# A state-space layer on one core: where the diagonal term, the zero fills and four norm vectors are loaded and issued, and the order of the stage's operations

## The chip, the cores and the metric

The kernel runs on one core of a Trainium2 chip. The metric is device time in microseconds (us) of one execution. A core has five engines that run side by side and wait for each other only through semaphores: TensorE (PE), VectorE (DVE), ScalarE (ACT), GpSimd (POOL) and SyncE (SP). Each works off its own queue in order. In this kernel SP issues nearly all loads; POOL issues the transfers that add to their destination.

## The reference

The model is one S5 state-space layer with a GLU and an MLP, then a shared key and value projection, one forgetting-attention layer with its MLP, and a final norm, on 512 tokens of 1024 channels in float32. The change lies in the first of these:

```python
def s5_mixer(u, log_dt, a_re, a_im, b_re, b_im, c_re, c_im, d_skip, w_glu):
    uf = u.reshape(bsz, length, N_GROUPS, SSM_GROUP)          # 64 groups of 16 channels
    lam_bar = jnp.exp(lam * dt)                                # 64 complex states in a group
    b_bar = ((lam_bar - 1.0) / lam)[..., None] * b
    bu = jnp.einsum('blgc,gpc->blgp', uf, b_bar)
    _, states = lax.associative_scan(_ssm_binop, (a_elems, bu), axis=1)
    y = jnp.real(jnp.einsum('blgp,gcp->blgc', states, c))
    y = y + d_skip.reshape(N_GROUPS, SSM_GROUP) * uf           # the diagonal term
    z = jax.nn.gelu(y.reshape(bsz, length, D_MODEL))
    zw = z @ w_glu
    return zw[..., :D_MODEL] * jax.nn.sigmoid(zw[..., D_MODEL:])
```

The input u of this function is the normalised x: x times its inverse root mean square times the vector mix_norm[0].

## The kernel before, in words

The sequence is cut into 64 chunks of 8 tokens (T = 8). Inside a chunk the layer is a small Toeplitz matrix over 8 tokens and 16 channels; between chunks a scan carries the state. The 64 groups are worked in 8 blocks (b = 0 to 7) of 8 groups.

A part in front of the blocks, in the order of the code, loads the parameters, builds the powers of lam_bar (LL, ML) and the transposed B and C (XY, four planes). Planes 1 and 3 of XY are planes 0 and 2 with the upper and lower 64 partitions exchanged; SP does that with two DMAs each (lines 344 and 345, `swap`), for groups 0 to 15 (`sw_0_0`, `sw_2_0`) and for the rest (`sw_0_1`, `sw_2_1`). VectorE multiplies plane 0 by the norm vector first (line 470, `gain`).

Then come the blocks' operations. Their order is written out by hand in the string ORDER, one name per operation with its block; each engine takes its own share of that list in order, so the list is the order of every queue. The names that matter here:

- LR, mR, gR, tk, rxv: VectorE's last preparations (powers, their products with the coefficients, the gain for groups 16 to 63, the angles' tables, the inverse root mean square rxy). xs: ScalarE scales x by rxy into xs.
- gn: TensorE transposes the tile gl (four norm vectors of later layers), ScalarE copies it to gains.
- win1, win2, wina and wo1, wo2, woa: for a block the matrices Win and Wout, two products on VectorE each and an addition by a DMA that POOL issues (line 348).
- u, us: transposes of xs on TensorE and their copies. pw, wt: transposes of Win and copies to WinT. pd: the chunks' inputs to the state. tab0, tab3, tabn: tables of cosines and sines (CS).
- pt, ks, kd, kw, tr: the block's Toeplitz matrix. pt multiplies on TensorE, ks copies it to ks, kd adds the diagonal term dgb (line 614, VectorE), kw writes it to a DRAM buffer (line 617), tr reads it back as a Toeplitz matrix with a shifting access pattern (line 625). The DRAM buffer has seven blocks of zeros in front, which kzero writes once (line 262).
- cd, da, scan, pp, padd: the scan between chunks. cd rotates into cc (one buffer); da exchanges halves, for blocks 0 to 3 with two matmuls, for blocks 4 to 7 with a pair of POOL's adding DMAs; scan is one VectorE instruction; pp rotates back; padd is a pair of adding DMAs.
- py1, py2: TensorE applies the Toeplitz matrix and Wout. gelu, zt, zh, lo: the activation, its transposes and the split into two float32r parts.
- gl_n, gs, gv, gp: three of the GLU's weight chunks are loaded, split and multiplied inside this stage.

ks needs pt, and kd needs dgb. dgb holds d_skip times mix_norm[0] on the diagonal places of a block: two sets of four small loads by SP (line 253, tiles dgb and dgg) and, as operation dg of the list, two VectorE multiplies.

The buffers for Wout come from two pairs A and B; the string WQ says which pair each takes. After the stage the rest of the GLU (line 834), the MLPs and the attention follow; their order is made by a planner that fills gaps of the list with matmuls that are ready.

Of the kernel before, what the change touches and what calls it, by code (L numbers as in the profile page):

```python
# [1592 lines left out]
```

## Time and profile before

| what | us |
|---|---|
| median of 3 runs | 1198.26 |
| lowest, highest | 1196.67, 1198.49 |
| the profiled execution's own time | 1196.73 |
| its span, from the first to the last instruction | 1195.0 |
| TensorE busy in the span | 1113.5 |
| VectorE busy | 908.3 |
| ScalarE busy | 588.5 |
| GpSimd busy | 291.4 |

The span is what the trace shows; the time of an execution holds 1.73 us more. A busy time counts an engine's instructions, not its waits. The state-space stage is the first eighth of the span: the last block's py2 starts at 148.63 us.

### The profile page before, as it was taken

The page shows a single profiled execution, that of the slowest core. Times are in us where ns is not written, and L with a number is a line of the kernel's source. Part 1 is how long each engine was busy: PE and PEld are TensorE (multiplying, and loading weights), DVE is VectorE, ACT ScalarE, POOL GpSimd, SP SyncE. Part 2 cuts the span into 40 slices and gives each one's busy share as a digit, 9 for nine tenths or more (in the row PEclk, how much of TensorE's full clock was granted, in tenths as well). Part 3 has the DMA queues.
Part 4 walks back from the last instruction along what each step waited for, and adds up shares of the span by engine and source line. Part 5 has one row for each costly group of instructions (what it writes and reads, how often), then busy time and mean ns, then how long its engine had stood idle before and what let it go on. Part 6 is the DMA issues. An engine that isn't in the chain of part 4 may idle for free.

```text
span 1195.0 us, 19068 instructions
## 1 busy us (share of the span) xinstructions
PE 1113.5 (93%) x7205; PEld 985.7 (82%) x7205; DVE 908.3 (76%) x1640; ACT 588.5 (49%) x1072; POOL 291.4 (24%) x290
## 2 busy tenths in 40 slices
PE   1687899999999999999999999888899999999997
PEld 1566778899899898998888999767889898999986
DVE  7988438899877777768566778885979877778754
ACT  4656355455434444436345666554755444443433
POOL 3134214422121212203002222314442312213101
PEclk9989999999999999999999999998999999999999
DMA  7889743142323323234145444311143323232222
GB/s 157 181 176 207 188 144 106 53 141 90 123 89 102 111 75 120 88 103 128 55 132 134 107 107 137 94 54 53 36 126 104 112 83 124 89 119 93 89 88 71
DMA packets 118140, 131.19 MB, mean 110 GB/s; under 512 B 15200, under 2 KB 98432, under 8 KB 118048
## 3 DMA queue, kind: packets, MB, share of 16 engines
q1 hardware_dynamic: 113824, 118.44, 33.6%
q0 software_dynamic: 4224, 11.54, 5.5%
q8 instruction: 57, 0.93, 0.3%
q14 instruction: 35, 0.29, 0.1%
HBM read 103.21 MB, written 3.60 MB: 89 GB/s over the span
## 4 chain that ended last, share of the span: by engine, by line
PE 75%; DVE 11%; DMA 5%; ACT 3%; SPq 3%; issue 2%; POOL 1%; DVEq 0%; ACTq 0%; POOLq 0%
PE pu L943 23%; PE po L834 16%; PE pvs L1508 14%; PE pk L834 6%; PE pv L834 6%; PE pvs L1154 2%; PE po L1292 2%; DMA PP<-PP 1%; DMA cc<-cc 1%; DMA st<-in_mlp_w_dram 1%; PE ptp L1258 1%; PE pf L1142 1%; DVE prob L1253 1%; DMA TW<-kd 1%; PE pw L834 1%
## 5 line engine op out<-in xcount | busy, mean ns | idle before, releaser
L943 PE MATMUL pu<-hm,ar 128*128 128x256 f32 x1536 | 229.0, 284 | 5.1 <-ACT hm L887 2.2
L943 PEld LDWEIGHTS pu<-hm,ar 128*128 128x128 f32 x1536 | 204.1, 193 | 6.7 <-ACT hm L887 2.6
L922 POOL TENSOR_TENSOR ar<-ar,st 128x256 f32<-128x256 f32 x62 | 81.8, 1320 | 414.2 <-DVE ar L918 373.1
L124 ACT ACTIVATE wt<-st 128x1024 fp32r<-128x1024 f32 x110 | 116.3, 1057 | 124.6 <-PE pu L943 27.2
L834 PE MATMUL po<-at,wt 128*128 128x512 f32 x768 | 176.9, 389 | 0.0
L1508 PE MATMUL pvs<-wt,at 128*128 128x512 f32 (+1 forms) x768 | 175.5, 388 | 0.0
L834 PEld LDWEIGHTS po<-at,wt 128*128 128x128 f32 x768 | 143.2, 188 | 29.1
L1508 PEld LDWEIGHTS pvs<-wt,at 128*128 128x128 f32 x768 | 142.6, 188 | 28.8
L128 DVE TENSOR_TENSOR wt<-st,wt 128x1024 fp32r<-128x1024 f32 x90 | 116.9, 1298 | 36.9 <-ACT wt L124 36.8
L943 PE MATMUL pu<-hd,x 128*128 128x256 f32 x768 | 136.0, 284 | 0.0
L911 ACT ACTIVATE ar<-ar 128x512 fp32r<-128x512 f32 x128 | 77.0, 627 | 91.6 <-PE pu L943 78.5
L943 PEld LDWEIGHTS pu<-hd,x 128*128 128x128 f32 x768 | 113.2, 192 | 2.9 <-issue 0.5
L912 DVE TENSOR_TENSOR ar<-ar 128x512 fp32r<-128x512 f32 x128 | 87.9, 692 | 31.4 <-ACT ar L911 31.3
L128 POOL TENSOR_TENSOR wt<-st,wt 128x1024 fp32r<-128x1024 f32 x20 | 48.2, 2410 | 143.7 <-ACT wt L124 133.9
L911 ACT ACTIVATE x<-st 128x512 fp32r<-128x512 f32 x62 | 36.4, 625 | 94.8 <-PE pvs L1508 45.0
L918 DVE TENSOR_TENSOR ar<-st 128x512 f32<-128x512 f32 x62 | 49.8, 806 | 39.3 <-DMA st<-in_mlp_w_dram 38.8
L834 PE MATMUL pv<-zt,wt 128*128 128x512 f32 x312 | 74.3, 397 | 0.4 <-ACT hT L1016 0.4
L834 PEld LDWEIGHTS pv<-zt,wt 128*128 128x128 f32 x312 | 59.2, 192 | 12.9 <-ACT hT L1016 0.6
L1244 ACT ACTIVATE prob<-psx,mx 128x128 f32<-128x128 f32 (+1 forms) x64 | 33.8, 529 | 60.5 <-DVE mx L1242 60.5
L1063 ACT ACTIVATE at<-c 128x512 fp32r<-128x512 f32 x64 | 39.8, 630 | 42.9 <-DVE c L1061 42.9
L923 POOL TENSOR_TENSOR ar<-ar,st 128x256 f32<-128x256 f32 x62 | 58.7, 950 | 4.2
L1049 DVE TENSOR_TENSOR hT<-hT,po 128x512 f32<-128x512 f32 x64 | 43.4, 679 | 16.1 <-PE po L834 16.1
(338 smaller groups left out, 1997.6 us busy)
## 6 DMA issues: line engine op xcount, KB each, us to landing
st<-in_mlp_w_dram SPq DMA_DIRECT2D x126, 512.0 KB
st<-in_ssm_w_glu_dram SPq DMA_DIRECT2D x16, 512.0 KB
st<-in_w_kvf_dram SPq DMA_DIRECT2D x14, 512.0 KB
hx<-kt SPq DMA_DIRECT2D x48, 128.0 KB
Win<-tB POOLq DMA_DIRECT2D x8, 512.0 KB, 5.5
TW<-tB POOLq DMA_DIRECT2D x8, 512.0 KB, 6.4
TW<-kd SPq DMA_DIRECT2D x32, 128.0 KB
st<-in_attn_wq_dram SPq DMA_DIRECT2D x8, 512.0 KB
```

The source lines that it names most:

```text
L124: S.activation(wt[:, 0], st, AF.Copy)
L128: (G if slot[1] == "A" and CFG["x"][7 + lows[0] % 3] == "G" else V).tensor_tensor(wt[:, 1], st, wt[:, 0].bitcast(F32), op=ALU.subtract)
L834: TE.matmul(pts[m], wt[:, a, k, m * P:(m + 1) * P], acts[k0 + k][:, b], start=(first and k0 == parts[0][0] and k == 0 and n == 0), stop=(k ...
L911: S.activation(X[0], src, AF.Copy)
L912: V.tensor_tensor(X[1], src, X[0].bitcast(F32), op=ALU.subtract)
L918: V.tensor_tensor(Ta[:, :, js].rearrange("p w j n -> p j w n"), f[:, :, 1:3], f[:, :, 0:1].broadcast_to([P, 2, 2, P]), op=ALU.add)
L922: e.tensor_tensor(Tb[:, 0, js], Ta[:, 0, js], v[:, :, 1, 0], op=ALU.add)
L923: e.tensor_tensor(Tb[:, 1, js], Tb[:, 0, js], v[:, :, 1, 1], op=ALU.add)
L943: TE.matmul(self.acc[p], self.W[p][:, a, j], self.H.moving(p, j, b), start=(p == g[0] and j == 0 and n == 0), stop=(p == g[-1] and j == 3 ...
L1049: V.tensor_tensor(hT[:, m, :], hT[:, m, :], po[j], op=ALU.add)
L1063: S.activation(at_[:, 0], c, AF.Square)
L1508: TE.matmul(po[:, cols], A[k][:, b], wts[k // 2][:, a, k % 2, cols], start=start and n == 0, stop=stop and n == 3 * len(ks) - 1)
```

## The change

The diagonal term is built in another way: one load dbc brings d_skip to all 128 partitions, and POOL multiplies the parts that belong to each quarter of the partitions with those of gbc (mix_norm[0], which is loaded for the gain anyway), and then with the mask. The operation dg disappears from VectorE's list, and so do SP's eight loads of dgb and dgg. The four zero fills of the DRAM buffers and the four loads of gl are issued by POOL, behind these multiplies, and the source of the zeros is a tile of full length, so that a partition's zeros are one run of 896 bytes. dbc takes a buffer of the tag WinT. The strings ORDER and WQ are replaced by new ones: the same operations but for dg, in another order.

```diff
-WQ = "AABBBABABB"
+WQ = "AABBABAABA"
 ORDER = """
-LR mR gn gl_0 gl_1 gl_2 gR win2V_0 sw_0_1 decS_1 tk sw_2_1 sw_2_0 rxv win1V_1 xsS_1_1 win1V_0 xsS_0_1 wo2V_0
-wina_0 wo1V_0 xsS_1_0 wo2V_1 woa_0 xsS_0_0 wo1V_3 u_6 u_3 win2V_1 u_2 u_0 usS_2 wo1V_1 wina_1 u_1 usS_6 u_4
-usS_1 win1V_2 woa_1 pw_0 usS_3 usS_0 taV u_5 wtS_0 tab0V_0 u_7 gs_0 pd_0 tab0V_1 tab3_0 win2V_2 pt_0 wo2V_2
-wina_2 usS_5 pw_1 usS_7 cd_0 ksS_0 wtS_1 wo1V_2 da_0 usS_4 win1V_3 woa_2 tab3_1 pt_1 dg pd_1 kd_0 tab0V_2 kw_0
-ksS_1 kd_1 tab3_2 win2V_3 kw_1 pw_2 cd_1 wina_3 wtS_2 wo2V_3 da_1 tab0V_4 woa_3 pt_2 tr_0 scan_1 tab3_4 pd_2
-pp_1 tr_1 decS_0 win2V_5 padd_1 tabn_4 pw_3 ksS_2 cd_2 wtS_3 scan_0 da_2 kd_2 decS_2 pp_0 kw_2 pd_3 padd_0
-scan_2 tab0V_3 decS_3 py1_0 win1V_4 tab3_3 pt_3 win2V_4 py1_1 ksS_3 wina_4 cd_3 py2_1 kd_3 tr_2 win1V_7 da_3
-gelu_1 pp_2 kw_3 wo1V_4 padd_2 zt_1 wo2V_4 py2_0 win1V_5 woa_4 gelu_0 pw_4 gs_2 win2V_6 wina_5 zt_0 wtS_4 gv_2
-zhS_0 scan_3 py1_2 zhS_1 tr_3 pp_3 decS_4 pd_4 lo_1 padd_3 lo_0 py2_2 cd_4 pt_4 gelu_2 wo1V_5 da_4 zt_2 ksS_4
-kd_4 win1V_6 gp_2_0 kw_4 zhS_2 lo_2 wina_6 pw_5 gv_0 gp_2_1 wtS_5 tab0V_5 wo2V_5 tab3_5 pd_5 wo2V_6 woa_5
-tab0V_6 py1_3 scan_4 tr_4 tabn_5 py2_3 tab3_6 cd_5 gp_0_0 wo1V_6 da_5 gelu_3 pw_6 pp_4 gp_0_1 woa_6 tabn_6
-win2V_7 decS_5 padd_4 pt_5 wtS_6 tab0V_7 zt_3 ksS_5 pd_6 wo2V_7 tab3_7 wina_7 kd_5 kw_5 py1_4 scan_5 tabn_7
-pp_5 decS_6 zhS_3 pt_6 cd_6 padd_5 ksS_6 lo_3 py2_4 kd_6 da_6 kw_6 gp_0_3 gelu_4 wo1V_7 woa_7 gp_0_2 tr_5 pw_7
-gp_2_3 wtS_7 pd_7 scan_6 tr_6 pp_6 decS_7 zt_4 cd_7 gp_2_2 padd_6 zhS_4 lo_4 pt_7 da_7 ksS_7 kd_7 py1_5 kw_7
-py2_5 py1_6 gelu_5 gs_1 py2_6 gv_1 zt_5 gelu_6 scan_7 zt_6 zhS_5 tr_7 gp_1_0 zhS_6 pp_7 lo_5 gp_1_1 padd_7
-lo_6 gp_1_2 gp_1_3 py1_7 py2_7 gelu_7 zt_7 zhS_7 lo_7
+LR tk gl_1 gl_0 gl_2 gR mR sw_0_1 decS_0 sw_2_1 sw_2_0 rxv win1V_0 xsS_1_1 win2V_0 xsS_0_1 wo2V_0 wina_0 gn
+wo1V_0 xsS_0_0 wo1V_2 woa_0 xsS_1_0 win2V_1 u_0 u_1 win1V_1 u_5 usS_0 u_4 taV wina_1 u_3 usS_4 u_6 tab0V_0
+usS_3 pw_0 usS_1 wo2V_1 tab3_0 u_7 wo1V_1 u_2 pt_0 tab0V_1 wtS_0 woa_1 usS_2 win2V_2 pd_0 ksS_0 usS_5 kd_0
+wo2V_2 kw_0 tab3_1 pw_1 cd_0 woa_2 tab0V_2 wtS_1 da_0 win1V_2 tab3_2 pd_1 scan_0 wina_2 tr_0 win1V_3 decS_1
+pt_1 usS_7 cd_1 ksS_1 gs_1 kd_1 da_1 pp_0 kw_1 usS_6 gs_0 win2V_3 padd_0 scan_1 wina_3 pw_2 pp_1 decS_2 pt_2
+wtS_2 tab0V_3 padd_1 ksS_2 py1_0 tab3_3 kd_2 win2V_5 kw_2 tr_1 pd_2 win1V_4 wo2V_3 py2_0 cd_2 pw_3 gelu_0
+win2V_4 da_2 tab0V_4 wina_4 wtS_3 wo1V_3 tr_2 tab3_4 zt_0 scan_2 woa_3 pd_3 pp_2 py1_1 cd_3 padd_2 tabn_4
+decS_3 win1V_5 da_3 zhS_0 lo_0 wina_5 wo2V_4 pw_4 scan_3 py2_1 wtS_4 tab0V_5 pd_4 gelu_1 wo1V_4 tab3_5 pp_3
+woa_4 pt_3 zt_1 cd_4 padd_3 py1_2 win1V_6 py2_2 da_4 tabn_5 wo2V_5 ksS_3 pw_5 gelu_2 kd_3 wo1V_5 kw_3 gv_1
+woa_5 decS_4 zt_2 zhS_1 win2V_6 pt_4 zhS_2 lo_1 wtS_5 wina_6 win1V_7 gp_1_0 ksS_4 kd_4 wo2V_6 kw_4 pd_5 tr_3
+scan_4 decS_5 gp_1_1 cd_5 pp_4 pt_5 da_5 ksS_5 gv_0 padd_4 pw_6 win2V_7 tr_4 kd_5 gp_0_0 tab0V_7 wtS_6 wina_7
+wo2V_7 tab3_7 pd_6 kw_5 lo_2 tab0V_6 py1_3 scan_5 tab3_6 py2_3 gp_0_1 wo1V_6 tabn_6 tabn_7 woa_6 cd_6 py1_4
+decS_6 gelu_3 pp_5 da_6 py2_4 pw_7 wo1V_7 gelu_4 tr_5 padd_5 zt_3 wtS_7 zt_4 zhS_3 woa_7 pd_7 lo_3 zhS_4 lo_4
+pt_6 gp_1_2 ksS_6 scan_6 gp_0_2 decS_7 cd_7 py1_5 pp_6 da_7 kd_6 py2_5 kw_6 padd_6 gp_0_3 gs_2 gelu_5 gv_2
+pt_7 ksS_7 gp_2_0 kd_7 kw_7 gp_2_1 scan_7 tr_6 zt_5 pp_7 gp_2_3 zhS_5 lo_5 padd_7 tr_7 gp_2_2 gp_1_3 py1_6
+py2_6 gelu_6 zt_6 py1_7 zhS_6 lo_6 py2_7 gelu_7 zt_7 zhS_7 lo_7
...
             DMA.dma_start(gbc, mix_norm[0].partition_broadcast(P))
             for h in range(2):
                 DMA.dma_start(cs_[:, :, h, :], (c_re, c_im)[h][0])
-            dgb = [sp.tile([P, NB, 2 * GC], F32, name="dgb"),
-                   bp.tile([P, NB, 2 * GC], F32, name="dgg", tag="dd", bufs=1)]
+            dgb = sp.tile([P, NB, 2 * GC], F32, name="dgb")
+            dbc = bp.tile([P, D], F32, name="dbc", tag="WinT", bufs=2)
+            DMA.dma_start(dbc, ssm_d[0].partition_broadcast(P))
 
             def xt(t):
                 return xth[t // 4][:, t % 4, :]
...
             mask = sp.tile([P, GC], F32, name="mask")
             for q in range(4):
                 G.tensor_copy(mask[q * 32:q * 32 + 32], ident[q * 32:q * 32 + 32, q * 32 + GC:q * 32 + 2 * GC])
-            zk = sp.tile([P, 64], F32, name="zk")
+            zk = sp.tile([P, (T - 1) * 32], F32, name="zk")
             G.memset(zk, 0.0)
             KD = [dp.tile([P, 2 * T - 1, 32], F32, name=f"kd{i}", tag=f"kd{i}", bufs=1) for i in range(4)]
 
-            def dl(i):
-                v = (ssm_d, mix_norm)[i][0][0:1]
-                for q in range(4):
-                    DMA.dma_start(dgb[i][q * 32:q * 32 + 32],
-                                  bass.AP(tensor=v.tensor, offset=v.offset + q * 32, ap=[[0, 32], [P, NB], [1, 32]]))
-
             def gnl():
                 for i, gsrc in enumerate((mlp_norm[0], kv_norm, mix_norm[1], mlp_norm[1])):
-                    DMA.dma_start(gl[i * KT:(i + 1) * KT, :], gsrc.rearrange("(k p) -> k p", p=P))
+                    G.dma_start(gl[i * KT:(i + 1) * KT, :], gsrc.rearrange("(k p) -> k p", p=P))
 
             def kzero():
                 for k in KD:
-                    DMA.dma_start(k[:, 0:T - 1], zk[:, 0:32].unsqueeze(1).broadcast_to([P, T - 1, 32]))
-
-            for i in range(2):
-                dl(i)
-            kzero()
-            gnl()
+                    G.dma_start(k[:, 0:T - 1].rearrange("p l n -> p (l n)"), zk)
+
             dtt = small("dtt")
             weave(exp_acc(dtt, ldt))
             ard, th, den, t3 = small("ard"), small("th"), small("den"), small("t3")
...
             weave(coef())
             mul_l(GA)
+            for q in range(4):
+                qs = slice(q * 32, q * 32 + 32)
+                G.tensor_tensor(dgb[qs], *[v.rearrange("p (b q n) -> p b q n", b=NB, q=4)[qs, :, q] for v in (dbc, gbc)],
+                                op=ALU.mult)
+            dv = dgb.rearrange("p b (g c) -> p (b g) c", c=GC)
+            G.tensor_tensor(dv, dv, mask.unsqueeze(1).broadcast_to([P, 2 * NB, GC]), op=ALU.mult)
+            kzero()
+            gnl()
 
             def m_chain(gs):
                 n = gs.stop - gs.start
...
             def b_kd(b):
                 d = KS[b][:, 0]
-                V.tensor_tensor(d, d, dgb[0][:, b].rearrange("p (g c) -> p g c", c=GC), op=ALU.add)
+                V.tensor_tensor(d, d, dgb[:, b].rearrange("p (g c) -> p g c", c=GC), op=ALU.add)
 
             def b_kw(b):
                 DMA.dma_start(KD[b % 4][:, T - 1:2 * T - 1].rearrange("p l n -> p (l n)"),
...
             def e_lo(b):
                 V.tensor_tensor(Z[b][:, 1], ZP[b], Z[b][:, 0].bitcast(F32), op=ALU.subtract)
 
-            def dg():
-                V.tensor_tensor(dgb[0], dgb[0], dgb[1], op=ALU.mult)
-                d = dgb[0].rearrange("p b (g c) -> p (b g) c", c=GC)
-                V.tensor_tensor(d, d, mask.unsqueeze(1).broadcast_to([P, 2 * NB, GC]), op=ALU.mult)
-
             def gn():
                 pg = pst("pg")
                 TE.transpose(pg[:, 0:4 * KT], gl, ident[0:4 * KT, 0:4 * KT])
...
```

## Rows read from the trace of the kernel before

**Rows 1.** Busy time by stage: stretch, then each engine's busy us (instructions), granted clock.
```profile
core 0: us, PE busy (x) PEld busy (x) DVE busy (x) ACT busy (x) POOL busy (x), PEclk, DMA share, GB/s
41.24:148.63 107.39, 91.53 (x990) 74.18 (x991) 85.09 (x109) 60.20 (x88) 33.75 (x46) 0.94 0.87 183
...
230.00:1195.00 965.00, 935.78 (x5769) 839.70 (x5767) 741.23 (x1363) 467.41 (x873) 217.96 (x175) 0.99 0.33 99
```

**Rows 2.** Chain of waits, 0 to 175 us: start, us, what.
```profile
26.63 0.29 SPq L258
...
27.58 2.00 DMA XY<-XY
...
36.29 4.90 ACT xs L562 x12
...
41.24 4.65 PE pu L574 x48
...
67.87 11.07 DMA TW<-kd
```

**Rows 3.** Timeline of SP: start, us, instructions merged (xcount).
```profile
12.71 6.85 SPq L253 DMA_DIRECT2D dgb<-in_ssm_d_dram  x4
...
27.02 0.51 SPq L344 DMA_DIRECT2D XY<-XY  x1
...
30.03 0.47 SPq L344 DMA_DIRECT2D XY<-XY  x1
...
34.65 0.60 SPq L345 DMA_DIRECT2D XY<-XY  x1
```

**Rows 4.** Timeline of VectorE, 20 to 55 us; in brackets idle time and what ended it.
```profile
20.36 0.42 DVE L470 TENSOR_TENSOR XY<-XY,gbc 128x256 f32<-128x256 f32 x1
20.69 1.02 DVE L477 TENSOR_TENSOR LL<-tmp 128x384 f32<-128x384 f32 x2
...
24.44 0.95 DVE L470 TENSOR_TENSOR XY<-XY,gbc 128x768 f32<-128x768 f32 x1
29.68 1.22 DVE L546 TENSOR_TENSOR tB<-ML,XY 128x1024 f32<-128x1024 f32 x1 [4.29 <-DMA XY<-XY]
30.82 0.42 DVE L457 TENSOR_SCALAR tk<-tAB 128x512 f32<-128x512 f32 x1
...
36.18 2.35 DVE L541 TENSOR_TENSOR Win<-ML,XY 128x1024 f32<-128x1024 f32 x2
40.88 1.23 DVE L546 TENSOR_TENSOR tB<-LL,XY 128x1024 f32<-128x1024 f32 x1 [2.35 <-DMA XY<-XY]
...
54.12 1.21 DVE L644 SCALAR_TENSOR_TENSOR cc<-cs,pd 128x1024 f32<-128x1024 f32 x1
```

**Rows 5.** Timeline of the late blocks: VectorE's waits, and TensorE's last py2.
```profile
81.44 1.23 DVE L644 SCALAR_TENSOR_TENSOR PP<-cs,tz 128x1024 f32<-128x1024 f32 x1 [2.46 <-PE py L692]
...
128.05 0.69 DVE L652 SCALAR_TENSOR_TENSOR cc<-cs,pd 128x512 f32<-128x512 f32 x1 [1.60 <-PE pd L639]
...
148.63 1.20 PE L692 MATMUL py<-TW,PP 128*64 128x64 f32 x32 [2.09 <-DMA PP<-PP]
```

**Rows 6.** Timeline of POOL: a multiply, the idle time before 29.51, a pair of issues.
```profile
11.16 1.08 POOL L309 TENSOR_TENSOR tAB<-f,jt 128x512 f32<-128x512 f32 x1 [4.88 <-DVE f L308]
...
29.51 0.11 POOL L632 MEMSET dec<- 128x8 f32 x1 [11.90 <-ACT dec L356]
...
67.70 1.65 POOL L348 DMA_DIRECT2D PP<-PP  x2
```

**Rows 7.** Timeline of VectorE, 15 to 19 us: the same kind of multiply twice.
```profile
15.13 0.43 DVE L425 TENSOR_TENSOR wi<-rr,tmp 128x64 f32<-128x64 f32 x1
...
18.15 0.20 DVE L441 TENSOR_TENSOR cr<-th,fr 128x64 f32<-128x64 f32 x1
```

**Rows 8.** Timeline of TensorE at 28 us: gn's transpose.
```profile
28.43 0.28 PE L730 MATMUL pg<-ident,gl 32*128 32x32 f32 x1 [3.88 <-DMA gl<-in_mlp_norm_dram]
```

**Rows 9.** Groups of TensorE's instructions by line, 41.2 to 149 us: busy us, mean ns.
```profile
L834 PE MATMUL pv<-zt,wt 128*128 128x512 f32 x10 | 2.7, 400 | 0.0
```

**Rows 10.** Timeline of ScalarE at 97 us.
```profile
97.51 1.28 ACT L372 ACT_TABLE_LOAD   x1
```

More of the change, by code (lines that the diff above doesn't have):

```diff
@@ L760, in body @@
                 "gl": g_load, "gs": g_s, "gv": g_v, "gp": g_pe,
-                "LR": partial(mul_l, GR, V), "mR": m_rest, "gR": lambda: gain(GR, V), "sw": sw, "rxv": rxv, "tk": lambda: weave(tk()), "ta": ta, "gn": gn, "dg": dg,
+                "LR": partial(mul_l, GR, V), "mR": m_rest, "gR": lambda: gain(GR, V), "sw": sw, "rxv": rxv, "tk": lambda: weave(tk()), "ta": ta, "gn": gn,
                 "tab0": tab0, "tab3": tab3, "tabn": tabn, "xs": make_xs, "u": u_pe, "us": u_s,
```

## The prediction

> **What bounds the kernel now.** I read the busy table by stage first. From 230 us to the end TensorE is busy 935.78 of 965 us [rows 1]; the change touches nothing there, so what it is worth is decided before. Between 41.24 and 148.63 us TensorE has 91.53 us of work in 107.39 us, so 15.9 us of idle time, and its clock is granted at 0.94 on the mean [rows 1].
>
> Second, the chain of waits for the first 175 us. Up to 27 us it lies on SP's issues alone; then it goes through a transfer that swaps halves of XY (2.00 us), the VectorE work behind it, ScalarE's xs copies (36.29) and TensorE's first u transposes at 41.24 [rows 2]. The reader is to see that TensorE starts its work at 41.24 because SP was late at 27.
>
> Third, the timeline of SP. The four loads of dgb begin at 12.71 and take 6.85 us; those of dgg, the zero fills of kd and the norm vectors follow, the last of these at 26.63 [rows 2], and only at 27.02 is the swap issued [rows 3]. VectorE had finished that swap's input at 20.78 (20.36 and 0.42) [rows 4]. So SP is 6.2 us late. VectorE, which has its own work until 25.39, then idles 4.29 us for the swap, and 2.35 us more at 40.88 for the last swap [rows 4].
>
> Fourth, what follows. Late in the stage blocks 4 to 7 go through one cc buffer, and there VectorE waits: for instance 1.60 us for pd at 128.05 [rows 5]. The last py2 starts at 148.63 behind a transfer [rows 5].
>
> **The change part by part.** The sum is against the profiled execution, 1196.73 us, of which the span is 1195.0; the median of the runs shown, 1198.26, lies 1.53 above it.
>
> *SP's queue.* Eight small loads, four zero fills and four vectors leave it; one broadcast load dbc of 512 KB comes in. dbc takes the place of the first dgb load and, like it, waits for room; the four dgb loads ended at 19.56 [rows 3], so I expect SP free by 20.8. The first swap then goes at 20.8 in place of 27.02, 6.2 us earlier.
>
> *VectorE up to rxy.* The new list puts LR, tk, gR, mR and rxv ahead of win1_0. In the trace LR, mR and gR run from 20.69 to 25.39 (4.70 us), tk and rxv from 30.82 to 36.29 (5.47) [rows 4, 2]. Without a wait between them they end at 20.69 + 10.17 = 30.86.
>
> *The multiplies on POOL.* Four of 32 x 256 and one of 128 x 256, in place of two on VectorE (0.42 us each by the 128 x 256 row [rows 4]). A 128 x 512 multiply on POOL took 1.08 us [rows 6]; for half the columns I take 0.6, so 3.0 us, about 24 to 27 us. POOL is idle for 11.90 us before 29.51 [rows 6], which hides its own time. VectorE pays: a 64-column multiply of two SBUF tensors took 0.43 us at 15.13, beside POOL's multiplies, and 0.20 at 18.15, when POOL had stopped [rows 7]. By this doubling 3.0 us of POOL cost VectorE 1.5 (0 if they fall into gaps, 3.0 at most). So rxv ends at 32.4, against 36.29.
>
> The Trainium skill's page "SBUF — State Buffer", section "Who interferes with whom", says that a VectorE instruction with two SBUF inputs and a GpSimd instruction that reads SBUF exclude each other for the whole instruction. By that the cost is all 3.0 us, rxv ends at 33.9, and the result below is about 0.5 smaller; the two rows show a doubling, and I keep 1.5.
>
> *POOL's eight DMA issues, and gn.* A pair of issues on POOL took 1.65 us [rows 6], so eight take 6.6 us. dbc lands about 24 if it takes the 5.6 us that the swap issued at 34.65 (0.60) needed to 40.88 [rows 3, 4], counted from its issue near 18. POOL is then through at 24 + 3.0 + 6.6 = 33.6. The next work behind it is the add of Win, wanted after win2_0 at about 32.4 + 2.35 = 34.8 [rows 4]: hidden. But gn, which needs gl, now stands in front of u_0 on TensorE and between the xs copies on ScalarE. When SP loaded gl the last issue ended at 26.92 [rows 2] and gn's transpose ran at 28.43 [rows 8], 1.5 us later; the 5.6 us above is the far bound. gl lands between 35.1 and 39.2; I take 36.0, since the pieces are 4 KB. With the transpose (0.28) and a small copy gn is through at 36.5. ScalarE has by then done two of its four groups of xs (4.90 us for 12 copies [rows 2], 1.63 for four: 32.4 + 3.3 = 35.7), waits 0.8 us, and finishes the third group, which releases u_0, at 38.1. Before it was 41.24: **lead 3.1 us**, bounds 0 (gl at 39.2) and 5.4 (no contention, no wait).
>
> *VectorE's second wait.* The last swap: six issues took from 30.03 to 35.25, and now start when gR ends, near 25.7, so it lands near 30.9 + 5.6 = 36.5. wo2_0 waits from 34.8 to 36.5 and starts 4.4 us earlier than at 40.88; one 1.2 us operation fewer stands in front, which leaves 3.2. VectorE and TensorE therefore lead by the same 3 us.
>
> *The order from cd_0 to scan_4.* VectorE is the bound there. Seven operations leave the stretch: dg (0.84), gv_0, gv_2 and wo1_2 (1.2 each, as 128 x 1024 at 54.12), lo_2 (0.69 by the 512-column row), tab0_6 (two of 0.69) and kd_0; gv_1, win1_2 and wo1_3 (3.6) enter it [rows 4, 5]. Net 2.9 us less. Lead at scan_4: 6.0.
>
> *The order in the tail.* cd_6 and cd_7 used to stand behind pp_5 and pp_6; now cd_7 follows scan_6 at once and pd_7 is further ahead. That saves pp_6 (two operations of 0.69) and the 1.60 us for pd [rows 5]: 3.0 us (bounds 0 and 4.5, with pp_5 too). Of the work pushed into the tail 3.3 us net lie under VectorE's own idle time (85.09 busy of 107.39 [rows 1]); without that cover they come back. The last py2 starts 9.0 us earlier.
>
> *What TensorE keeps.* Its work is the same. Ten matmuls of the following projection (2.7 us [rows 9]) filled gaps before 148.63; if the gaps go, they come later: minus 2.7. Needed is an idle time 3.2 us shorter of 15.9, which is there. The new list alternates Sin and Gelu seven times, the old one five; a table load is 1.28 us [rows 10], ScalarE is busy 60.20 of 107.39 [rows 1], so half of two shows: minus 1.3.
>
> Sum: 3.1 + 2.9 + 3.0 - 2.7 - 1.3 = **5.0 us faster**: 1191.7 for the profiled execution, 1193.3 for the median.
>
> **Rivals.** *Same: the wait moves to POOL's queue.* dbc, five multiplies and eight issues in one row make gl land at 39 or later; u_0 then starts at 41.2 and TensorE, busy in most of the stage, gives the tail's gain back. For it: nothing on POOL can overtake, and each step above had a late bound. Time: lead 0, order +3.2 of idle time, loads -1.3: within 2.4 us of before, 1196 to 1200.
>
> *Slower: wo1_3 waits for py2_0.* In the new list the third Wout goes into the buffer of Wout_0, which py2_0 frees, and stands in VectorE's queue in front of all that follows. VectorE would reach it 17 operations of about 1.15 us and two short ones after cd_0 (54.12 - 3.1 = 51.0), at 71. py2_0 needs block 0's Toeplitz read: kd_0 at about 50, the landing of its write (5.6 as the swap), four issues (0.6 each, as at 34.65 [rows 3]), up to 11.07 for the read [rows 2], 3 for py1 and py2: 72. In the trace VectorE waited 2.46 us for the first py2, at 81.44 [rows 5]. If py2_0 ends after 76 the gain is gone, after 78.4 the kernel is slower; ending as late as before, at 81.4, VectorE loses 10.4 us and the result is 5.4 us slower, 1203.7. Against it: block 0 goes alone here, where eight reads of two blocks were issued together.
>
> *More: TensorE's clock comes back too.* With mean 0.94 over 107.39 us [rows 1] some 6.4 us are lost to the lower level. If the gaps in front of these stretches close, 5.0 + 6.4 = 11.4 faster, 1186.9. Against it: 12.7 us of idle time remain by my sum.
>
> That the swap isn't earlier at all would need SP blocked by dbc until 27; dbc has 128 long rows where the loads that blocked had short ones, so I give it no case of its own.
>
> **How the numbers follow.** A change within 0.2% (2.4 us) can't be told from none. Forecast 0.50 (its own range 2.4 to 8.6 faster, the upper end being 5.4 + 2.9 + 3.0 - 2.7: 1189.7 to 1195.9), more 0.15, same 0.18, slower 0.17. Faster is 0.65. The range for 8 in 10 runs from 1186, past the case with the clock, to 1200, the end of the case without change; it leaves out the slower case and a little below.
>
> **What would show it.** In the new profile: the first swap issued near 20.8 and no VectorE idle time of 4 us behind it; rxy near 32.4; dbc's multiplies on POOL between 24 and 27 and VectorE's operations beside them longer; gl's last issue near 33.6 and gn's transpose near 36; u's first transpose near 38; scan_4 some 6 us earlier than before; the last py2 near 140. Wrong it would be by a ScalarE wait of several us in front of gains, by a VectorE wait in front of wo1_3 for py, or by a TensorE idle time that is no shorter although the last py2 comes earlier.

## The result and the profile after

Before: 1197.82 us median of five runs (1194.40 to 1198.49). After: 1188.87 us (1187.83 to 1191.40). The ratio is 0.9941, 95% interval 0.9915 to 0.9966: 7.1 us faster (4.1 to 10.2). The forecast was 5.0. The profiled execution took 1187.83 us with a span of 1186.1, against 1195.0: 8.9 less; it is the fastest of its five executions, so some of the 8.9 is their spread.

Busy time by stage of the changed kernel, cut at u's first transpose and at the last py2 (compare [rows 1]):
```profile
core 0: us, PE busy (x) PEld busy (x) DVE busy (x) ACT busy (x) POOL busy (x), PEclk, DMA share, GB/s
0.00:38.56 38.56, 5.40 (x39) 4.56 (x39) 33.36 (x109) 18.62 (x41) 21.30 (x58) 1.00 0.80 198
38.56:143.81 105.25, 89.82 (x1002) 73.66 (x1004) 82.28 (x106) 62.25 (x90) 33.51 (x46) 0.94 0.87 189
...
230.00:1186.10 956.10, 929.94 (x5706) 834.89 (x5704) 734.34 (x1340) 462.12 (x862) 209.17 (x172) 0.98 0.33 99
```
The stage starts 2.68 us earlier and is 2.14 shorter. TensorE's idle time in it is 15.43 us, against 15.86: hardly less.

Timeline of SP after (compare [rows 3]): one load, and the first swap at 21.17 in place of 27.02.
```profile
13.31 5.33 SPq L167 DMA_DIRECT2D dbc<-in_ssm_d_dram  x1
21.17 0.51 SPq L335 DMA_DIRECT2D XY<-XY  x1
...
30.31 1.43 SPq L336 DMA_DIRECT2D XY<-XY  x1
```
Timeline of VectorE after (compare [rows 4]): no wait of 4 us behind gR (the gain of 768 columns), none in front of wo2_0 at 35.69 (2.35 before, at 40.88), and cd_0 at 49.02 in place of 54.12.
```profile
21.99 0.42 DVE L448 TENSOR_SCALAR tk<-tAB 128x512 f32<-128x512 f32 x1
...
25.73 1.48 DVE L461 TENSOR_TENSOR XY<-XY,gbc 128x768 f32<-128x768 f32 x1
27.13 1.07 DVE L485 TENSOR_TENSOR ML<-LL,cr 128x384 f32<-128x384 f32 x1
28.12 1.07 DVE L485 TENSOR_TENSOR tmp<-LL,ci 128x384 f32<-128x384 f32 x1
29.12 0.55 DVE L485 TENSOR_TENSOR ML<-LL,ci 128x384 f32<-128x384 f32 x1
...
33.33 0.17 DVE L511 SCALAR_TENSOR_TENSOR rxy<-rxu,rxy 128x8 f32<-128x8 f32 x1
...
35.69 1.22 DVE L545 TENSOR_TENSOR tB<-LL,XY 128x1024 f32<-128x1024 f32 x1
...
49.02 1.21 DVE L643 SCALAR_TENSOR_TENSOR cc<-cs,pd 128x1024 f32<-128x1024 f32 x1
```
Timeline of POOL after (compare [rows 6]): the multiplies take 5.2 us, not 3.0, and the issues 0.5 to 0.6 each, not 0.8.
```profile
23.48 4.30 POOL L474 TENSOR_TENSOR dgb<-dbc,gbc 32x256 f32<-32x256 f32 x4 [5.91 <-DMA dbc<-in_ssm_d_dram]
27.87 0.92 POOL L477 TENSOR_TENSOR dgb<-dgb,mask 128x256 f32<-128x256 f32 x1
28.73 2.44 POOL L257 DMA_DIRECT2D kd<-zk  x4
...
32.67 0.50 POOL L253 DMA_DIRECT2D gl<-in_mlp_norm_dram  x1
```
While these multiplies ran, VectorE's operations were longer: the 768-column gain took 1.48 us (0.95 in [rows 4]), a 384-column product 1.07 beside POOL and 0.55 behind it. Over all of them that is 2.3 us.

Timeline of TensorE after, the start and the late blocks (compare [rows 5] and [rows 8]):
```profile
35.76 0.28 PE L724 MATMUL pg<-ident,gl 32*128 32x32 f32 x1 [10.72 <-DMA gl<-in_mlp_norm_dram]
38.56 4.28 PE L573 MATMUL pu<-ident,xs 64*128 64x64 f32 x48 [2.53 <-ACT xs L561]
42.77 1.75 PE L589 MATMUL pw<-ident,Win 128*128 128x128 f32 x8
44.45 1.01 PE L573 MATMUL pu<-ident,xs 64*128 64x64 f32 x16
...
120.97 0.45 PE L691 MATMUL py<-TW,Uall 128*64 128x64 f32 x8 [2.29 <-DMA TW<-kd]
121.79 0.45 PE L691 MATMUL py<-TW,Uall 128*64 128x64 f32 x8 [0.36 <-DMA TW<-kd]
122.64 0.70 PE L691 MATMUL py<-TW,Uall 128*64 128x64 f32 x8 [0.40 <-DMA TW<-kd]
...
137.18 5.29 PE L828 MATMUL pv<-zt,wt 128*128 128x512 f32 x22
...
143.81 1.10 PE L691 MATMUL py<-TW,PP 128*64 128x64 f32 x32
```
py1_5 is the last instruction that waits for a Toeplitz read; from 122.64 to the last py2 TensorE has no gap, and 22 matmuls of the following projection (5.3 us, ten and 2.7 in [rows 9]) already stand in front of that py2. The chain of waits says the same of the 20 us before:
```profile
102.54 7.14 DMA TW<-kd
109.72 1.39 PE py L691 x40
...
114.62 7.97 DMA TW<-kd
122.64 2.40 PE py L691 x40
```

**A sum over TensorE, and why it isn't a cause.** The 8.9 us can be booked on TensorE: start 2.68; idle time 0.43; its own work without the projection 4.3 less (91.53 - 2.7 = 88.8 against 89.82 - 5.3 = 84.5, for the same 980 matmuls); 2.6 more of the projection carried inside; and from the last py2 to the MLP's first group of 96 matmuls in the chain of waits (239.00, before 247.59) 95.19 us in place of 98.96, 3.77 less: 2.68 + 0.43 + 4.3 - 2.6 + 3.8 = 8.6, so only 0.3 is left for the rest. The 4.3 is a matter of pace. From u to da_0 the rows of the same matmuls add up to 18.1 us before and 12.9 after; in the kernel before they kept half pace for 16 us:
```profile
47.72 1.97 PE L574 MATMUL pu<-ident,xs 64*128 64x64 f32 x16
49.62 3.67 PE L639 MATMUL pd<-Uall,WinT 128*128 128x64 f32 x16
```
In the changed kernel these are 1.01 and 2.00. Whether this pace set the end is what the last experiment bears on: there the slow pace came back and the kernel was no slower.

### The profile page after: what moved, and what is told of

Same layout as the page of the kernel before. It is cut to its first block, busy times and chain, and to the rows that moved or that the text cites. A ratio compares the mean times of both kernels' runs of the same rounds, so it can differ in the third digit from the quotient of the medians.

```text
span 1186.1 us, 19074 instructions
## 1 busy us (share of the span) xinstructions
PE 1109.2 (94%) x7205; PEld 984.6 (83%) x7205; DVE 911.7 (77%) x1638; ACT 589.9 (50%) x1074; POOL 294.9 (25%) x303
## 4 chain that ended last, share of the span: by engine, by line
PE 80%; DVE 9%; DMA 5%; ACT 3%; issue 2%; SPq 1%; DVEq 0%; ACTq 0%
PE pu L937 25%; PE po L828 16%; PE pvs L1502 15%; PE pk L828 6%; PE pv L828 6%; PE pvs L1148 2%; PE po L1286 2%; DMA Win<-tB 1%; DMA TW<-kd 1%; PE ptp L1252 1%; PE pf L1136 1%; DMA bc<-in_ssm_b_im_dram 1%; DVE prob L1247 1%; PE py L691 1%; PE pw L828 1%
## 5 line engine op out<-in xcount | busy, mean ns | idle before, releaser
L916 POOL TENSOR_TENSOR ar<-ar,st 128x256 f32<-128x256 f32 x62 | 75.2, 1215 | 422.6 <-DVE ar L912 383.4
L128 DVE TENSOR_TENSOR wt<-st,wt 128x1024 fp32r<-128x1024 f32 x90 | 116.2, 1293 | 35.6 <-ACT wt L124 35.2
L917 POOL TENSOR_TENSOR ar<-ar,st 128x256 f32<-128x256 f32 x62 | 59.3, 958 | 4.2
L1057 ACT ACTIVATE at<-c 128x512 fp32r<-128x512 f32 x64 | 39.7, 630 | 38.1 <-DVE c L1055 38.1
```

The source lines that it names most:

```text
L128: (G if slot[1] == "A" and CFG["x"][7 + lows[0] % 3] == "G" else V).tensor_tensor(wt[:, 1], st, wt[:, 0].bitcast(F32), op=ALU.subtract)
L916: e.tensor_tensor(Tb[:, 0, js], Ta[:, 0, js], v[:, :, 1, 0], op=ALU.add)
L917: e.tensor_tensor(Tb[:, 1, js], Tb[:, 0, js], v[:, :, 1, 1], op=ALU.add)
L1057: S.activation(at_[:, 0], c, AF.Square)
```

## The experiments

Each ratio is against the kernel before on the same chip, as is the 0.9941 of the changed kernel. The edits are to the changed kernel if nothing else is said.

**1. The loads alone** (new loads, multiplies and issues; old ORDER and WQ without dg).
```diff
-ORDER = """ (new)
+ORDER = """ (old, without dg)
```


> The new loads and POOL's multiplies and issues with the old order and the old string of buffers (the entry for the diagonal product, which has moved to POOL, taken out of the list). Theory A (the two parts add: the loads free SP, the order saves work between the first and the fifth scan): the swap goes near 21 instead of 27.0, VectorE's idle time of 4.3 us at 29.7 goes, and the old order gives some of it back since it has the transpose of the norm vectors in front: gl lands near 35.5, ScalarE's xs copies start near 36.0 as before. 1 to 4 us faster than before, 5 to 8 slower than the changed kernel. Theory B (the order does it alone): within 1 us of before. Theory C (the loads do it alone): 7 to 9 us faster than before.

1196.43 us, ratio 1.0000 (0.9985 to 1.0016): no gain. The swap went at 20.95 and VectorE's wait was gone, but the old list has gn ahead of the xs copies, and POOL's four multiplies took 7.23 us here. Timeline of ScalarE in this kernel:
```profile
38.02 0.20 ACT L725 ACTIVATE gains<-pg 128x32 f32<-128x32 f32 x1 [12.02 <-PE pg L724]
```
ScalarE waited 12.02 us for gl; the xs copies began at 38.63 and u at 43.56, later than before. This is the rival "the wait moves to POOL's queue", come true under the old order.

**2. The order alone** (old loads on SP; new ORDER and WQ, dg in front of kd_0).
```diff
-... usS_5 kd_0
+... usS_5 dg kd_0
```


> The new order and buffer string with the old loads on SP and the diagonal product on VectorE, in front of the first use. Theory A: the swaps land late (the last near 40.8), VectorE has all its preparations done near 31.2 and then waits some 5 us in front of wo2_0; TensorE's first transposes start early, near 36, since rxy is early and gl is there. 2 to 5 us faster than before, 4 to 7 slower than the changed kernel. Theory B (the order does it alone): 7 to 9 us faster than before. Theory C (the loads do it alone): within 1 us of before.

1199.49 us, ratio 1.0028 (1.0009 to 1.0046): 3.4 us slower. Timeline of VectorE in this kernel:
```profile
43.40 1.23 DVE L546 TENSOR_TENSOR tB<-LL,XY 128x1024 f32<-128x1024 f32 x1 [10.28 <-DMA XY<-XY]
```
u came as early as 35.90, but the last swap was issued at 34.86, landed at 43.3, and VectorE stood for it. So neither part gains by itself, and an account that adds up two gains is wrong: the list needs the early swaps, and the loads, with gl on POOL's queue, need gn behind the first xs copies.

**3. The multiplies on VectorE** (in front of kd_0; POOL issues at once).
```diff
-            for q in range(4): G.tensor_tensor(dgb[qs], ...)
+            def dg(): for q in range(4): V.tensor_tensor(dgb[qs], ...)
```


> The changed kernel with the five multiplies of the diagonal term on VectorE, as an operation in front of the first use, and POOL's eight issues right after its last power. In the changed kernel VectorE's operations beside POOL's multiplies took 2.3 us more than alone. If the sharing costs what the rows show, rxy comes near 31.3 instead of 33.5 and TensorE's first transposes near 36.4 instead of 38.6; VectorE pays some 2 us for the five multiplies later. Theory that the start sets the end: 1 to 2 us faster than the changed kernel. Rival that VectorE's sum of work up to the fifth scan sets the end: the same as the changed kernel within 1 us.

1192.53 us, ratio 0.9964 (0.9945 to 0.9983). u came at 36.37, 2.2 earlier than in the changed kernel, and wo2_0 at 33.87; but VectorE then did 2.1 us of multiplies, waited 1.51 for ks and 1.15 for pd_0, and cd_0 came at 52.11, 3.1 later. The span is 2.7 longer. An earlier u did not help here, where cd_0 was later; that the kernel is slower than the changed one isn't clear of noise, since the two intervals overlap.

**4. Fills and norm vectors on SP** (in front of the first swap).
```diff
-                    G.dma_start(gl[i * KT:(i + 1) * KT, :], ...)
+                    DMA.dma_start(gl[i * KT:(i + 1) * KT, :], ...)
-                    G.dma_start(k[:, 0:T - 1]...)
+                    DMA.dma_start(k[:, 0:T - 1]...)
```


> The changed kernel with the four zero fills and the four norm vectors issued by SP again, behind the broadcast load and in front of the swap; the multiplies stay on POOL. SP's issues of these eight took 5.1 us in the trace of before, so the swap goes near 24 instead of 21.2. Theory that the new order has already taken the need for the early swap away (VectorE wants its first product only at 34.5, and the last swap is issued behind the gain of the other groups anyway): within 1 us of the changed kernel. Rival that taking these eight off SP was part of the gain: 2 to 4 us slower than the changed kernel.

1188.33 us, ratio 0.9941 (0.9917 to 0.9964), the span 1186.1: the time of the changed kernel. The first swap went at 23.16, 2.0 later, yet wo2_0 waited only 0.65 us and cd_0 came at 49.34. Under the new order this move is worth nothing.

**5. The same under the old order.**
```diff
-ORDER = """ (new)
+ORDER = """ (old, without dg), with the edit of 4
```


> The old list of operations with the one broadcast load and POOL's multiplies, the zero fills (in their long runs) and the norm vectors back on SP in front of the first swap. In the first experiment ScalarE's xs copies began at 38.6 us because gn stood first and waited for norm vectors that POOL issued last. Here the vectors land before 27 us. Theory A, only gl on POOL's queue ate the gain of the new loads: first swap near 23.2, rxy near 33, xs near 33.5, u near 38.5, cd_0 near 51, 2 to 4 us faster than the kernel before. Theory B, the earlier start is lost again under the old list whatever the start is, since its tail waits for other things: u near 38.5 all the same, and less than 1.2 us faster than before.

1194.24 us, ratio 0.9966 (0.9947 to 0.9985): theory A, 4.1 us faster (1.8 to 6.3). Timeline of TensorE in this kernel:
```profile
39.68 4.64 PE L573 MATMUL pu<-ident,xs 64*128 64x64 f32 x48 [14.50 <-ACT xs L561]
```
Against experiment 1 only the queue of eight small issues differs: on POOL behind its multiplies they cost the loads' whole gain (the two intervals just touch). Against experiment 4 only the list and the string of buffers differ, and there the intervals overlap (0.9917 to 0.9964): what the new list adds to loads issued in this way isn't shown.

**6. Short fills** (experiment 4 with runs of 128 bytes).
```diff
-  DMA.dma_start(k[:, 0:T - 1].rearrange("p l n -> p (l n)"), zk)
+  DMA.dma_start(k[:, 0:T - 1], zk[:, 0:32].unsqueeze(1).broadcast_to([P, T - 1, 32]))
```


> The changed kernel with fills and norm vectors on SP (as in the fourth experiment), and the zero fills written in runs of 128 bytes in place of long ones: the same bytes in many more packets, the same number of issues in the same order. Theory A, the short runs keep the DMA engines busy and that is what makes the swaps behind them land late (43.3 us where the new list ran with the old loads): SP issues at the same times as in the fourth experiment, but the last swap lands 2 to 6 us later, VectorE waits as much for it in front of wo2_0, and the kernel is 1 to 4 us slower than in the fourth experiment. Theory B, only the place in SP's queue counts, not the length of the runs: last swap lands near 36, 1188.3 us as in the fourth experiment.

1191.98 us, ratio 0.9959 (0.9943 to 0.9975); the span 4.2 longer than in 4. SP's issues were slower as well (first swap at 24.77, the last at 31.89 in place of 30.60), and wo2_0 waited 2.76 us, until 38.04. That is theory A's direction, but of the 2.0 us by which wo2_0 went later 1.3 come from the later issue, which theory A did not have, and the intervals of 4 and 6 overlap. It leaves most of the 43.3 us of experiment 2 unexplained: there the short loads of dgb and dgg stood in front too.

**7. One multiply on POOL** (without the mask and the choice of columns, so its output isn't the layer's).
```diff
-            for q in range(4): G.tensor_tensor(dgb[qs], ...)
-            G.tensor_tensor(dv, dv, mask...)
+            G.tensor_tensor(dgb..., dbc[:, 0:NB * 2 * GC], gbc[:, 0:NB * 2 * GC], op=ALU.mult)
```


> The changed kernel with one 128x256 multiply on POOL in place of the four of 32x256 and the one with the mask (the diagonal term takes wrong columns and has no mask, so the output is not the reference's; all loads, issues and the order stay). POOL's 5.2 us beside VectorE become about 0.9, and the eight issues behind them go 4 us earlier. Theory A, VectorE's path through cd_0 sets the end of the stage and POOL's multiplies stretch it by 2.3 us: rxy near 31.4, cd_0 near 47, 1.5 to 3 us faster than the changed kernel. Theory B, TensorE's work is full by then and the stretch is covered: rxy near 31.4 too, but less than 0.8 us faster.

1188.76 us, ratio 0.9928 (0.9908 to 0.9947), the span 0.8 shorter than in the changed kernel. rxy ended at 31.7, 1.8 earlier, u came 1.8 earlier, and it was given back at once (timeline of VectorE):
```profile
35.56 1.23 DVE L540 TENSOR_TENSOR tB<-LL,XY 128x1024 f32<-128x1024 f32 x1 [1.55 <-DMA XY<-XY]
...
48.90 1.21 DVE L638 SCALAR_TENSOR_TENSOR cc<-cs,pd 128x1024 f32<-128x1024 f32 x1
```
Theory A's mechanism fell, and theory B's reason too: without POOL's 2.3 us of contention VectorE stands for the last swap until 35.56, and in the changed kernel it reaches the same operation at 35.69 without a wait.

**8. scan_7 in front of gv_2.**
```diff
-... gelu_5 gv_2 / pt_7 ksS_7 gp_2_0 kd_7 kw_7 gp_2_1 scan_7 tr_6
+... gelu_5 scan_7 gv_2 / pt_7 ksS_7 gp_2_0 kd_7 kw_7 gp_2_1 tr_6
```


> The changed kernel with scan_7 moved in front of gv_2, which stood on VectorE for 6.94 us and waited for a buffer while scan_7's input was done. Theory A, TensorE is full from 130 us on and the chain in the tail no longer decides: the last scan starts 3 to 6 us earlier, the last py2 as well, fewer matmuls of the following projection stand in front of it, and the time stays within 1 us of the changed kernel. Theory B, the chain through scan_7 and the last py2 sets the end: 2.5 to 5 us faster than the changed kernel.

1188.44 us, ratio 0.9928 (0.9904 to 0.9952), the span 1186.2. scan_7 came 4.2 us earlier (124.10) and the time stayed: theory A. Its by-product did not come: the last py2 began at 145.25, not earlier. TensorE has the same full queue in front of it: the 218 matmuls from py1_5's last piece to the last py2 took 22.40 us without a gap, at a granted clock of 0.86 (the mean over its two levels), and 21.17 in the changed kernel, at 0.92.

**9. A shorter start** (slices gathered by ScalarE, two POOL multiplies behind the issues, one swap issued by ScalarE).
```diff
-sw_2_1 sw_2_0 rxv
+swS_2_1 sw_2_0 dg rxv
+  S.activation(o[qs], v...[qs, :, q], AF.Copy)   # dbc and gbc, q = 0 to 3
+  G.tensor_tensor(dgb, dgb, dgg, op=ALU.mult)
```


> The changed kernel with the start of the stage shortened at both places that hold VectorE there: the eight slices of dbc and gbc are gathered by ScalarE (idle from 26.6 to 33.5 us) and POOL does two 128x256 multiplies in place of five behind its eight DMA issues, and one of the last three swaps is issued by ScalarE, not SP. In the seventh experiment rxy came 2.0 us earlier, but VectorE then waited 1.55 us for the last swap. Theory A, these two are the whole bound of the start and the lead then runs through: rxy near 31.5, wo2_0 near 34, cd_0 near 47.3 (1.7 earlier than in the changed kernel), 1 to 2 us faster than the changed kernel. Theory B, the lead is lost to the Toeplitz reads of blocks 3 to 5 in the middle: cd_0 as early, less than 0.8 us faster.

1188.02 us, ratio 0.9924 (0.9895 to 0.9953); the span 1188.2. rxy ended at 30.7 and u came at 35.77, 2.8 earlier, but the last swap landed at 35.6 again (wo2_0 waited 1.55) although its last issue began at 28.40. pd_0 ran at half pace (3.67) and cd_0, at 49.60, waited 0.58 for it. So theory A's way fell; what holds the swap is not SP's issue, and it stays open what does. A rival that no run tests: three loads of 512 KB are issued by SP just in front of it (21.97 to 23.69), and the DMA share reads 1.05 from 24 to 28 us and 1.03 from 28 to 32; from 32 to 36 it is 0.20.

**10. Block 3's Toeplitz read earlier.**
```diff
-wtS_5 wina_6 win1V_7 gp_1_0 ksS_4 kd_4 wo2V_6 kw_4 pd_5 tr_3
+wtS_5 wina_6 win1V_7 tr_3 gp_1_0 ksS_4 kd_4 wo2V_6 kw_4 pd_5
-tab3_7 pd_6 kw_5 lo_2 tab0V_6 py1_3 scan_5 tab3_6 py2_3
+tab3_7 py1_3 py2_3 pd_6 kw_5 lo_2 tab0V_6 scan_5 tab3_6
```


> The changed kernel with the Toeplitz read of block 3 issued before the write of block 4's values (tr_3 ahead of kd_4 and kw_4) and py1_3 and py2_3 ahead of pd_6 on TensorE. In the changed kernel SP spent 12.4 us from 91.4 on eight issues, block 5's write stood behind them until 104.4, its read landed at 122.6, and TensorE has no gap behind that read. Theory A, this chain of writes and reads sets the end of the stage: the piece of py1_5 that waits longest starts near 119 to 121 in place of 122.6, 1 to 3 us faster than the changed kernel. Theory B, the reads have no effect on the end, because TensorE's work, not its gaps, fills the stage: within 0.8 us of the changed kernel, or slower where SP, waiting for block 3's write, holds back block 4's.

1192.00 us, ratio 0.9954 (0.9931 to 0.9977), the span 5.8 longer. Timeline of SP here, and of TensorE:
```profile
90.27 4.22 SPq L624 DMA_DIRECT2D TW<-kd  x4
94.59 0.46 SPq L113 DMA_DIRECT2D st<-in_ssm_w_glu_dram  x1
95.15 0.53 SPq L616 DMA_DIRECT2D kd<-ks  x1
105.16 3.76 SPq L624 DMA_DIRECT2D TW<-kd  x4
...
117.50 0.69 PE L691 MATMUL py<-TW,Uall 128*64 128x64 f32 x8 [3.47 <-DMA TW<-kd]
```
In this execution the second half of theory B came true: block 4's write went 4.3 us later (95.15 against 90.88), its read at 105.16, and py1_4's last piece began 7.8 us later (117.50 against 109.72). That the delay costs time isn't shown: the twelve executions lie between 1187.45 and 1196.21 us, this one took 1193.71, and the interval overlaps that of the changed kernel. Hastening the chain wasn't achieved.

**11. Both.** The edits of 9 and 10 together.
```diff
(the edits of experiments 9 and 10)
```


> Both edits of the ninth and tenth kernel together. If the start and the Toeplitz chain bound in series, the gains add: 2 to 5 us faster than the changed kernel. If one of them covers the other, as fast as the better of the two.

1187.44 us, ratio 0.9927 (0.9899 to 0.9954): no better than 9, so there are no gains that add. Block 4's write went as late as in 10 (94.81), yet the last piece of py1_4 that waits for its read began at 109.05, not 117.50 (timeline of TensorE):
```profile
109.05 2.08 PE L686 MATMUL py<-TW,Uall 128*64 128x64 f32 x24 [0.30 <-DMA TW<-kd]
```
So the late write alone doesn't explain 10; what delayed its read stays open.

**12. cd_6 and cd_7 behind pp_5 and pp_6**, as in the old list.
```diff
-cd_6 py1_4 / decS_6 gelu_3 pp_5 da_6     and  cd_7 py1_5 pp_6 da_7
+py1_4 / decS_6 gelu_3 pp_5 cd_6 da_6     and  py1_5 pp_6 cd_7 da_7
```


> The changed kernel with cd_6 and cd_7 put back behind pp_5 and pp_6, as they stood in the old list; nothing else. The prediction counted 3.0 us for this part of the new order, because the scans of blocks 6 and 7 would come earlier by it. Theory A, as predicted: scan_6 and scan_7 start 1.2 to 2.6 us later and the kernel is 2 to 3 us slower than the changed one. Theory B, the scans stand behind other things (the Toeplitz reads, the buffer that gv_2 waits for) and TensorE is full from 130 us on: py1_5 still ends near 123, the last py2 near 144, and the time is within 0.8 us of the changed kernel.

1186.88 us, ratio 0.9924 (0.9903 to 0.9945): theory B. Timeline of TensorE in this kernel:
```profile
46.76 3.68 PE L638 MATMUL pd<-Uall,WinT 128*128 128x64 f32 x16
...
122.95 0.45 PE L691 MATMUL py<-TW,Uall 128*64 128x64 f32 x8 [1.14 <-DMA TW<-kd]
...
142.88 1.10 PE L691 MATMUL py<-TW,PP 128*64 128x64 f32 x32
```
It shows a second thing. Here pd_0 ran at half pace (3.68 against 2.00), and from u to da_0 TensorE needed 16.8 us, 3.9 more than in the changed kernel; from u to the last py2 its busy time was 92.58 of 104.78 us, the idle time 12.2. The slower matmuls mostly filled idle time: cd_0 waited 1.73 us for pd_0 and came 1.45 later (50.47), py1_5's last piece 0.31 later, and the kernel was as fast. One reserve: from that piece to the last py2 the granted clock was 1.00 here and 0.92 in the changed kernel (19.93 us and 21.17), so some 1.2 us of the term may be covered in this profile.

No kernel beats the changed one by more than the intervals allow: 0.9924 to 0.9941 for the seven of 4, 7, 8, 9, 11, 12 and itself.

**What the runs have in common.** In the kernels with the new order of the Toeplitz reads (all but 1, 5, 10 and 11), the end goes with the last piece of py1_5, which waits for block 5's Toeplitz read (us; spans of the profiled executions):
```
kernel       cd_0    py1_5's last piece   last py2   span
2 order      57.76   133.84               155.53     1198.0
6 fills      52.05   127.21               148.25     1190.3
3 on VectorE 52.11   124.78               145.96     1188.8
9 start      49.60   123.62               144.66     1188.2
12 cd        50.47   122.95               142.88     1185.7
8 scan_7     49.29   122.85               145.25     1186.2
changed      49.02   122.64               143.81     1186.1
7 one mult.  48.90   122.28               143.48     1185.3
4 fills SP   49.34   121.56               142.73     1186.1
```
From 121.56 to 133.84 (12.3 us) the span goes from 1186.1 to 1198.0 (11.9), and from that piece to the end it is 1062.8 to 1064.6 us in all nine. From cd_0 to the piece it is 72.2 to 76.1, so only the large differences of cd_0 (experiments 2, 3 and 6) can be followed; the other six lie within the spread. Experiment 11, with its reads in another order, has 122.88 and a span of 1182.2; that profile is the fastest of its six executions, and its ratio is no better. The reading that fits: behind py1_5 TensorE is full, so what comes later there is hidden; in front of it, VectorE's path through cd_0 counts, and u's start counts only as far as cd_0 follows it. No run moves cd_0 and nothing else, so this path is argued from the table, not shown.

## Why the prediction was right, point by point

**SP's queue: right.** 21.17 us against 20.8 expected.

**VectorE up to rxy: the contention was mis-sized.** rxv ended at 33.5, not 32.4. POOL's five multiplies took 5.2 us in place of 3.0 (the 32 x 256 ones 1.07 each, as long as a 128 x 512 one [rows 6]), and cost VectorE 2.3 in place of 1.5. The doubling read from [rows 7] held: 2.3 of 5.2 is near the half that I took; the term failed by the duration. The Trainium skill's page "SBUF — State Buffer", section "Who interferes with whom", by which the two engines exclude each other for the whole instruction, would give 5.2; the trace shows 2.3: VectorE's operations took 1.6 to 2.0 times as long as alone, and none was longer by a whole POOL multiply of 1.07.

**POOL's issues and gn: right in sum.** Multiplies longer, issues shorter (4.5 us in place of 6.6): the last at 32.67 to 33.17, gn's transpose at 35.76, no ScalarE wait in place of 0.8. u at 38.56 where 38.1 was forecast, lead 2.7 for 3.1.

**VectorE's second wait: mis-sized.** No wait in place of 1.7, and the 1.2 us that I took off for an operation fewer in front of wo2_0 was not lost up to cd_0: wo2_0 to cd_0 takes 13.24 us before and 13.33 after. VectorE's lead at cd_0 is 5.1, not 3. Experiments 7 and 9 show that u's lead by itself brings nothing (u 1.8 and 2.8 earlier, the time the same). That cd_0's counts is clear of noise only in experiment 2, where it came 8.7 us later than in the changed kernel; so "lead 3.1" was put, it seems, on the wrong engine.

**From cd_0 to scan_4: the work was right, the waits were left out.** VectorE's busy time there fell from 45.08 to 42.03, 3.05 where 2.9 was forecast; its waits fell from 3.67 to 0.87 us (the 2.46 for py2 of [rows 5] among them). Lead at scan_4 10.95, not 6.0 (timelines of VectorE, the kernel before and then the changed one):
```profile
102.87 1.22 DVE L675 TENSOR_TENSOR_SCAN tz<-cc,dec 128x512 f32<-128x512 f32 x1
```
```profile
91.92 1.22 DVE L674 TENSOR_TENSOR_SCAN tz<-cc,dec 128x512 f32<-128x512 f32 x1
```

**The tail: this step failed.** Forecast: 3.0 earlier, the last py2 9.0 earlier at about 140. Measured: from scan_4 to the last py2 51.89 us in place of 45.76; the lead sinks to 4.8. From scan_4 on TensorE still had 45.04 us of work (500 matmuls) up to the last py2, against 35.71 (403) before: VectorE had run ahead of it, and the forecast took VectorE's lead for the whole stage's. Experiment 12 takes the term away alone and loses nothing; experiment 8 brings scan_7 4.2 us forward for nothing. The scans of blocks 6 and 7 no longer decide; by the profile the last wait is that for block 5's Toeplitz read, and then TensorE's queue is full.

**What TensorE keeps: the sign was wrong.** I let ten projection matmuls (2.7 us) move behind the last py2; instead 22 stood in front, and from there to the MLP it took 3.8 us less. The sum also needed 3.2 us less idle time; it fell by 0.43, and an idle time no shorter with an earlier last py2 is what the prediction named as a sign of being wrong. In its place the same 980 matmuls took 4.3 us less (from u to da_0 alone 5.2 less), and experiment 12 shows work and idle time trading places. The table loads: seven in place of five, as counted; no run isolates their price.

**The sum: near by luck in part.** Forecast were 9.0 us up to the last py2 and 4.0 taken off; the profiles show 4.8 up to there and 4.1 more behind it, 8.9. One part is 4.2 too large and the other 8.1 too small. The direction rests on steps that held (the earlier swap and u, and the work saved from cd_0 to scan_4); the size does not.

**The rivals.** "Same" lost under the new order and came true under the old one (experiment 1). "Slower" didn't come: wo1_3 began at 69.82 with no wait for py; block 0's read was in time. "More": the mean granted clock in the stage stayed at 0.94. The early half pace that shortened is not in that column, which reads 1.00 in that stretch for both kernels, and in experiment 12, where it is long again, the kernel is no slower.

## What to carry to other kernels

A reordered list and an earlier transfer can be worth nothing apart and 7 us together: test each half before adding their gains, and test it again when one wait has been taken out of the way (experiment 5 got 4.1 us with the old list). Ask of every lead where it ends: here a lead on TensorE's first instruction died in VectorE's wait for a swap, and a lead in the tail died in a queue that was already full. A small load moved to an idle engine's queue inherits everything that stands in front of it there.

## What was not expected of the hardware

A POOL multiply of 32 x 256 took 1.07 us, one of 128 x 512 1.08 [rows 6] and one of 128 x 256 0.92 (0.73 in experiment 7): a quarter of the partitions saved nothing. Nor did it on VectorE, where four of 32 x 256 took 1.70 us and one of 128 x 256 0.43 (experiment 3). Beside other VectorE work POOL's four took 7.23 us (experiment 1). Whether the columns gathered from 1024 play a part, no run separates. In the changed kernel small plain transfers cost POOL 0.50 to 0.61 us to issue.

TensorE's first matmuls of the stage took twice as long as later ones of their kind, after 12.5 us of idle time in the kernel before (41.24), and in the changed one after 2.5 behind a single transpose (0.28) with 10.72 idle before it: for 16.3 us there, 5.9 here, with no idle time in either stretch and the granted clock at 1.00, the higher of its two levels, throughout. The Trainium skill's page "TensorE: Matmul & The Clock Gate", section "Part 1: The HAM clock gate (the "warmup" mystery)", says that an idle TensorE falls to half its clock and that the length of the way back varies from run to run; the doubling agrees with it, but the column of the granted clock doesn't show it, and one stretch three times the other is more than the variation that the section states. What makes the difference stays open. It isn't the idle time in front alone: in experiment 4 that was 12.94 us, and the stretch was as short as in the changed kernel (timeline of TensorE):
```profile
38.14 4.28 PE L573 MATMUL pu<-ident,xs 64*128 64x64 f32 x48 [12.94 <-ACT xs L561]
42.35 1.77 PE L589 MATMUL pw<-ident,Win 128*128 128x128 f32 x8
44.05 1.02 PE L573 MATMUL pu<-ident,xs 64*128 64x64 f32 x16
```
The busy times by stage of the two stretches, the kernel before and then the changed one:
```profile
41.24:57.58 16.34, 16.34 (x115) 14.34 (x115) 16.34 (x18) 11.83 (x21) 4.03 (x5) 1.00 0.79 150
```
```profile
38.56:44.45 5.89, 5.89 (x56) 5.60 (x57) 5.89 (x8) 4.54 (x9) 1.50 (x2) 1.00 0.99 188
```
